# Layer 0's output stage re-stepped, its follow-ups queued, and root rows spread by transposes

## The chip, the cores and the metric

The kernel runs on one core of one Trainium2 chip. The metric is the device time of the program in microseconds (us); lower is better. TensorE (PE) does the matrix products, VectorE (DVE) and ScalarE (ACT) the elementwise work, SyncE (SP) issues the DMA transfers.

## The reference

Two layers of a mixer on 1024 latent tokens and 256 context tokens, width 1024. Each layer normalises its input, projects it with one large matrix, runs three branches (differential attention, a long convolution, a gated MLP), merges them, projects the merge with `w_out`, normalises that and adds it to the stream. What matters here is the end of layer 0 and the start of layer 1:

```python
h  = rms_norm(x,  norm_pre[l]) * (1.0 + sc) + sh      # start of a layer, latents
hc = rms_norm(xc, norm_pre[l]) * (1.0 + scc) + shc    # and context
...
out = merge_branches(z, (y_a, y_b, y_c), w_branch[l], w_out[l])
x_new = x + gt * rms_norm(out, norm_post[l])          # end of a layer, latents
xc = xc + gtc * rms_norm(outc, norm_post[l])          # and context, layer 0 only
```

Inside attention every head's output is normalised by the same kind of root mean square.

## The kernel before

**Layout.** Activations lie with channels on the 128 partitions and tokens along the free axis, in three chunks of tokens: chunk 0 and chunk 1 (512 latents each) and chunk 2 (256 context tokens). Every product is made of three single-pass products of split operands (`mm3`, L178): high part by high part, high by low, low by high. A weight block (128 output channels, all 1024 inputs) is loaded by SP into `wr` (two buffers, L83), its high part `wh` is copied by ACT (L100) and its low part `wl` is the difference, taken by DVE (L101); both have two buffers. `Weights.get` hands a block out, `Weights.ahead` splits the next one.

**Order of the work.** The program is written as generators that yield between pieces, and are stepped against each other by hand; a scheduler then fixes one list of instructions for each engine, and each engine runs its list in order. So an instruction that waits holds back all that stands behind it on its engine.

**Layer 0's output stage** (`phase_o`). `out(c)` makes, for one chunk, eight blocks of 128 output channels: 24 products on PE (tile `po`), a copy `ot` and a square by ACT (L1248, L1250) and a running sum of squares by DVE (L1252). The chunk's follow-up `tail(c)` then takes the root of the mean square (`mean_rsqrt_steps`, tiles `msq`, `mn`, `mrb`), scales `ot` (L1225), adds the old stream (`xt`, L1227), stores it, and makes the input of layer 1 from it: squares and their sum (`hroot_steps`, L323 and L325), a second root, and `hnorm_steps`: scaled copy `ht` (L344), high part `hh` by ACT (L346), low part `hl` by DVE (L347). The follow-up of a chunk is stepped once a block beside the products of the next chunk, and what is left of it is run off (`drain`) before the chunk after that. Its steps are large: four channel blocks of `ot` and `xt` at a time, eight squares in one step, four of `hnorm` in one step. Chunk 2 reuses the last two weight blocks and splits six new ones.

**The fills.** After chunk 2's products come three blocks of layer 1's input projection (`o_fill`, tile `pd`, result `zz` stored by SP), each for chunk 0 and then chunk 1, beside the follow-up of chunk 2. Layer 1's `phase_a` then loads its rotary tables (`ropeC`, `ropeS`, L553 and L554), and `kvq` makes the first head's keys (tile `pd` for chunks 0, 1 and 2), queries and values. The keys' results go through `rope` (L392 to L395) on DVE. In `phase_a` the tile `pd` has two buffers, so the third chunk's product waits for the first one's rotary step.

**Spreading a root.** `mean_rsqrt_steps` has the roots of 128 tokens as one column (`mn`); to have them along the free axis on all partitions it multiplies the column, repeated 128 times, by the identity (`mrb`, L215). Attention does that twice per 256 queries and head, the output stage four times per 512 tokens and root. `gate_row` in `phase_last` does the same with eight columns (L1325).

Of the kernel before, what the change touches and what calls it, by code (L numbers as in the profile page):

```python
# [166 lines left out]
class Kernel:  # L167
# [31 lines left out]
    def mean_rsqrt_steps(self, pool, psum, ss, n, width, tag="P"):  # L199


        nc = self.nc
        nt = n // 128
        ps = psum.tile([128, 512], F32, name="msq", tag=tag)
        for t in range(nt):
            nc.tensor.matmul(ps[:, 2 * t:2 * t + 2], lhsT=ss[:, 128 * t:128 * t + 128], rhs=self.ones[:, 0:2],
                             start=True, stop=True)
        m = pool.tile([128, 12], F32, name="mn", tag="mn", bufs=2)
        x, r, t = m[:, 0:nt], m[:, 4:4 + nt], m[:, 8:8 + nt]
        nc.vector.tensor_scalar(out=x, in0=ps[:, 0:2 * nt:2], scalar1=1.0 / width, scalar2=EPS, op0=MUL, op1=ADD)  # L210
        self.rsqrt(r, x, t)
        yield
        pr = psum.tile([128, 512], F32, name="mrb", tag=tag)
        for t in range(nt):
            nc.tensor.matmul(pr[:, 128 * t:128 * t + 128], lhsT=r[:, t:t + 1].to_broadcast([128, 128]), rhs=self.ident,  # L215
                             start=True, stop=True)
        return pr[:, 0:n]

    def chunks(self, l):
# [96 lines left out]
    def hroot_steps(self, c, xt, pool, psum, tag="P"):  # L316
        nc = self.nc
        n = CHUNKS[c][1]
        ss = pool.tile([128, 512], F32, name="ss", tag="ss")[:, 0:n]
        for k in range(KT):  # L320
            sq = ss if k == 0 else pool.tile([128, 512], F32, name="sq", tag="sq")[:, 0:n]
            for s, x in xt(k):
                nc.scalar.activation(out=sq[:, s], in_=x, func=AF.Square)  # L323
            if k:
                nc.vector.tensor_tensor(out=ss, in0=ss, in1=sq, op=ADD)  # L325
        yield
        return (yield from self.mean_rsqrt_steps(pool, psum, ss, n, D, tag))

    def hnorm_steps(self, l, c, xt, r, pool, tag=None):

        nc = self.nc
        n = CHUNKS[c][1]
        j = 1 if c == 2 else 0
        mod = self.mod[l, 0]
        hh, hl = self.alloc_h(c)
        for k in range(KT):
            if tag is None:
                t = pool.tile([128, 512], F32, name="ht", tag="sq")[:, 0:n]
            else:
                if k % 4 == 0:  # L340
                    t4 = pool.tile([128, 4, 512], F32, name="ht", tag=tag)
                t = t4[:, k % 4, 0:n]
            for s, x in xt(k):
                nc.vector.scalar_tensor_tensor(out=t[:, s], in0=x, scalar=mod[:, 8 + k, j:j + 1], in1=r[:, s],  # L344
                                               op0=MUL, op1=MUL)
            nc.scalar.activation(out=hh[:, k, :], in_=t, func=AF.Identity, bias=mod[:, k, j:j + 1])  # L346
            nc.vector.scalar_tensor_tensor(out=hl[:, k, :], in0=t, scalar=mod[:, k, j:j + 1],  # L347
                                           in1=hh[:, k, :].bitcast(F32), op0=ADD, op1=SUB)
            if k == 3:
                yield  # L350
        self.hT[c] = (hh, hl)

# [192 lines left out]
    def phase_a(self, l):  # L545
        nc = self.nc
        with ExitStack() as st:
            P = st.enter_context(self.tc.tile_pool(name=f"pa{l}", bufs=1, reuse_waits="tile"))
            psum = st.enter_context(self.tc.tile_pool(name=f"psa{l}", bufs=1, space=PSUM, reuse_waits="tile"))
            psum = PsumTags(psum, {"S": 1, "T": 2, "O": 1, "P": 2})  # L550
            self.ropeC = P.tile([128, SEQ], F32, name="ropeC")
            self.ropeS = P.tile([128, SEQ], F32, name="ropeS")
            nc.sync.dma_start(out=self.ropeC, in_=self.A["rope"][:, 0, :])  # L553
            nc.sync.dma_start(out=self.ropeS, in_=self.A["rope"][:, 1, :])  # L554

            rest = self.ada_rest(P) if l == 0 else iter(())
            for h in range(HEADS):
                drain(self.kvq(l, h, P, psum))
                fill = chain(*[self.block(("in", l, BLK_HY + b), self.chunks(l), psum, self.evac_z(P, self.zd[l], b))
                               for b in self.hy_fill[l][h]],  # L560
                             *[self.block(("in", l, BLK_GM + b), self.chunks(l), psum, self.evac_z(P, self.gm[l], b))
                               for b in (2 * h, 2 * h + 1)])
# [643 lines left out]
    def phase_o(self, l):  # L1206
        nc = self.nc
        gg = self.mod[l, 1]
        with ExitStack() as st:
# [5 lines left out]
            def tail(c, ot, ss):  # L1215
# [8 lines left out]
                for k in range(KT):  # L1224
                    nc.vector.scalar_tensor_tensor(out=ot[:, k, :], in0=ot[:, k, :], scalar=gg[:, k, j:j + 1], in1=r,  # L1225
                                                   op0=MUL, op1=MUL)
                    nc.vector.tensor_tensor(out=xt[:, k, :], in0=ot[:, k, :], in1=xt[:, k, :], op=ADD)  # L1227
                    if k % 4 == 3:
                        nc.sync.dma_start(out=dst[:, k - 3:k + 1, t0:t0 + n], in_=xt[:, k - 3:k + 1, :])
                        yield  # L1230
                xk = whole(xt)
                r = yield from self.hroot_steps(c, xk, P, psum, "N")
                yield from self.hnorm_steps(l + 1, c, xk, r, P)

            def out(c):
                t0, n = CHUNKS[c]
# [4 lines left out]
                for d in ds:  # L1241
                    w = self.ws.get(("out", l, c, d))
                    ps = psum.tile([128, 512], F32, name="po", tag="P")
                    for k in range(KT):
                        self.mm3(ps[:, 0:n], (w[0][:, k, :], w[1][:, k, :]), (mh[:, k, :], ml[:, k, :]),
                                 k == 0, k == KT - 1)
                    self.ws.ahead()
                    nc.scalar.activation(out=ot[:, d, :], in_=ps[:, 0:n], func=AF.Copy)  # L1248
                    sq = ss if d == ds[0] else P.tile([128, 512], F32, name="sq", tag="sq")[:, 0:n]
                    nc.scalar.activation(out=sq, in_=ps[:, 0:n], func=AF.Square)  # L1250
                    if d != ds[0]:
                        nc.vector.tensor_tensor(out=ss, in0=ss, in1=sq, op=ADD)  # L1252
# [4 lines left out]
            back = None  # L1257
            for c in self.chunks(l):
                for w in out(c):
                    if back is not None:  # L1260
                        next(back, None)
                drain(back)
                back = self.tails.pop()
            for b in self.o_fill:
                for i, w in enumerate(self.block(("in", l + 1, BLK_HY + b), self.chunks(l + 1), psum,
                                                 self.evac_z(P, self.zd[l + 1], b))):
# [14 lines left out]
    def phase_last(self, l):  # L1281
# [4 lines left out]
        with ExitStack() as st:  # L1286
# [34 lines left out]
            def gate_row():  # L1321
                for a in range(2):
                    ps = psum.tile([128, 512], F32, name="gr", tag="N")
                    for i in range(4):
                        nc.tensor.matmul(ps[:, 128 * i:128 * i + 128], rhs=self.ident, start=True, stop=True,  # L1325
                                         lhsT=gg[:, 4 * a + i, 0:1].to_broadcast([128, 128]))
# [55 lines left out]
    def order(self):  # L1382
        o = []
        o += [("in", 0, BLK_HY + b) for b in self.s_fill]
        for l in range(DEPTH):
            for h in range(HEADS):
                o += [("in", l, BLK_K + h), ("in", l, BLK_Q + h), ("in", l, BLK_V + h)]
                o += [("in", l, BLK_HY + b) for b in self.hy_fill[l][h]]
# [342 lines left out]
```

## Time and profile before

| | us |
|---|---|
| median of 3 runs | 3040.4 |
| lowest and highest | 3034.4 and 3042.98 |
| the profiled execution's own time | 3040.74 |
| its span (first to last instruction) | 3039.0 |
| PE busy / DVE busy / ACT busy in the span | 2964.2 / 1944.0 / 1225.0 |

Busy time of PE counts any matmul in flight; PE's clock has two levels, 1.2 and 2.4 GHz, and the profile gives the mean granted clock of a stretch as a share of the higher one. A float32 product with the identity shows as two weight loads and two matmul records, a transpose as one of each.

### The profile page before, as it was taken

Reading aid. Unit: us, or ns where it says so; the run is one execution under the profiler, and the core shown is the slowest. Engines: PE = TensorE matmul, PEld = TensorE weight load, DVE = VectorE, ACT = ScalarE, POOL = GpSimd, SP = SyncE. Lnnn points to the kernel's source line nnn. Section 1 sums busy time; section 2 is a strip of 40 time slices with the busy share of each in tenths; the row PEclk is TensorE's granted clock in tenths of the full one; section 3 lists DMA queues with packets and bytes.
Section 4 is the critical chain, followed back from the end, with each engine's and each line's share of the span. In section 5 each row is a group of like instructions: output and inputs, shape, how many; then the busy total and the mean of one; then the engine's idle time right before and its main releaser. Section 6 shows DMA issues by size and latency. Waiting matters only on the chain.

```text
span 3039.0 us, 43277 instructions
## 1 busy us (share of the span) xinstructions
PE 2964.2 (98%) x16220; PEld 2501.2 (82%) x16220; DVE 1944.0 (64%) x4458; ACT 1225.0 (40%) x2037; POOL 0.2 (0%) x4
## 2 busy tenths in 40 slices
PE   8999999999999999999999999999999999999998
PEld 4888888888888887888887788888887877788888
DVE  6856777777866766235657766566666877635464
ACT  4533535353532332233334444545455333223241
POOL 0000000000000000000000000000000000000000
PEclk9999999999999999999999999999999999999999
DMA  7324131313365656354443321111114756647342
GB/s 256 135 102 130 55 98 59 100 63 92 111 219 184 208 177 198 109 165 149 130 162 118 118 68 58 65 61 56 63 60 139 218 177 203 204 152 228 94 142 84
DMA packets 243378, 395.76 MB, mean 130 GB/s; under 512 B 23582, under 2 KB 127902, under 8 KB 241888
## 3 DMA queue, kind: packets, MB, share of 16 engines
q1 hardware_dynamic: 243168, 392.99, 40.1%
q8 instruction: 128, 2.10, 0.3%
q14 instruction: 82, 0.67, 0.1%
HBM read 285.81 MB, written 97.65 MB: 126 GB/s over the span
## 4 chain that ended last, share of the span: by engine, by line
PE 85%; DVE 7%; DMA 6%; ACT 1%; issue 1%; SPq 0%; DVEq 0%; ACTq 0%
PE pd L180 16%; PE pd L182 16%; PE pd L181 16%; PE S L452 5%; PE pb L181 3%; PE pb L182 3%; PE pb L180 3%; PE T L489 2%; PE po L182 2%; PE po L180 2%; PE po L181 2%; PE ip L703 2%; DMA aw<-in_ada_wT 2%; PE O L180 1%; PE O L181 1%; PE O L182 1%
## 5 line engine op out<-in xcount | busy, mean ns | idle before, releaser
L180 PE MATMUL pd<-hh,wh 128*128 128x512 f32 (+1 forms) x2784 | 1045.3, 376 | 9.0 <-DVE r L393 2.9
L181 PE MATMUL pd<-hl,wh 128*128 128x512 f32 (+1 forms) x2784 | 1031.5, 371 | 0.2 <-DVE hl L368 0.2
L182 PE MATMUL pd<-hh,wl 128*128 128x512 f32 (+1 forms) x2784 | 1029.3, 370 | 0.7 <-DVE wl L101 0.7
L180 PEld LDWEIGHTS pd<-hh,wh 128*128 128x128 f32 x2784 | 527.6, 190 | 89.9 <-issue 6.0
L182 PEld LDWEIGHTS pd<-hh,wl 128*128 128x128 f32 x2784 | 527.1, 189 | 84.6 <-DVE wl L101 1.6
L181 PEld LDWEIGHTS pd<-hl,wh 128*128 128x128 f32 x2784 | 528.2, 190 | 77.1 <-issue 0.9
L101 DVE TENSOR_TENSOR wl<-wr,wh 128x1024 fp32r<-128x1024 f32 (+1 forms) x204 | 223.6, 1096 | 209.6 <-ACT wh L100 206.0
L100 ACT ACTIVATE wh<-wr 128x1024 fp32r<-128x1024 f32 (+1 forms) x204 | 195.2, 957 | 286.7 <-PE pd L181 182.1
L459 ACT ACTIVATE e<-S,sm 128x1280 f32<-128x1280 f32 (+1 forms) x144 | 177.7, 1234 | 178.0 <-DVE sm L457 143.8
L456 DVE TENSOR_REDUCE sm<-S 128x1 f32<-128x1280 f32 (+1 forms) x144 | 197.2, 1369 | 67.8 <-PE S L452 67.2
L180 PE MATMUL pb<-gh,wh 128*128 128x512 f32 (+1 forms) x480 | 177.4, 370 | 1.3 <-ACT gh L196 1.3
L181 PE MATMUL pb<-gl,wh 128*128 128x512 f32 (+1 forms) x480 | 177.7, 370 | 0.4 <-DVE gl L197 0.3
L182 PE MATMUL pb<-gh,wl 128*128 128x512 f32 (+1 forms) x480 | 177.3, 369 | 0.0
L452 PE MATMUL S<-K,q 128*128 128x512 f32 (+1 forms) x400 | 149.1, 373 | 6.9 <-ACT e L459 6.8
L1045 ACT ACTIVATE ev<-pd 128x512 f32<-128x512 f32 (+1 forms) x122 | 66.7, 546 | 170.8 <-PE pd L182 113.7
L452 PE MATMUL S<-K,w 128*128 128x512 f32 (+1 forms) x400 | 135.3, 353 | 0.0
L197 DVE TENSOR_TENSOR pl<-T,ph 128x512 fp32r<-128x512 f32 x164 | 109.5, 687 | 28.1 <-ACT ph L196 26.3
L196 ACT ACTIVATE ph<-T 128x512 fp32r<-128x512 f32 x164 | 94.3, 597 | 67.9 <-PE T L489 67.8
L290 DVE SCALAR_TENSOR_TENSOR at<-aw,acs 128x256 f32<-128x256 f32 x224 | 88.5, 421 | 40.6 <-DMA aw<-in_ada_wT 37.9
L468 DVE SCALAR_TENSOR_TENSOR e<-e,sm,e 128x1280 f32<-128x1280 f32 (+1 forms) x72 | 102.7, 1426 | 6.2 <-ACT e L467 5.7
L452 PEld LDWEIGHTS S<-K,q 128*128 128x128 f32 x400 | 75.0, 187 | 38.3 <-ACT e L459 24.7
L489 PE MATMUL T<-ident,e 128*128 128x128 f32 x656 | 104.3, 276 | 0.6 <-DVE pl L197 0.3
(390 smaller groups left out, 4594.9 us busy)
## 6 DMA issues: line engine op xcount, KB each, us to landing
wr<-in_w_in SPq DMA_DIRECT2D x136, 512.0 KB, 3.5
fm<-in_fmat SPq DMA_DIRECT2D x99, 192.0 KB, 3.1
fm<-in_imat SPq DMA_DIRECT2D x72, 256.0 KB, 2.9
sel<-sd SPq DMA_DIRECT2D x70, 256.0 KB, 2.7
aw<-in_ada_wT SPq DMA_DIRECT2D x128, 128.0 KB, 2.5
wr<-in_w_out SPq DMA_DIRECT2D x28, 512.0 KB, 3.3
sd<-ev SPq DMA_DIRECT2D x50, 256.0 KB, 2.3
zd<-zz SPq DMA_DIRECT2D x48, 256.0 KB, 2.0
```

Of the source, the lines that this page charges most:

```text
L100: nc.scalar.activation(out=hi[:, 0:k, :], in_=t[:, 0:k, :], func=AF.Copy)
L101: nc.vector.tensor_tensor(out=lo[:, 0:k, :], in0=t[:, 0:k, :], in1=hi[:, 0:k, :].bitcast(F32), op=SUB)
L180: mm(out, lhsT=wh, rhs=xh, start=first, stop=False)
L181: mm(out, lhsT=wh, rhs=xl, start=False, stop=False)
L182: mm(out, lhsT=wl, rhs=xh, start=False, stop=last)
L196: nc.scalar.activation(out=hi, in_=src, func=AF.Copy)
L197: nc.vector.tensor_tensor(out=lo, in0=src, in1=hi.bitcast(F32), op=SUB)
L452: nc.tensor.matmul(S[:, a - k0:b - k0], lhsT=st[:, o + 128 * t:o + 128 * t + 128], rhs=K[m][:, a:b], start=i == 0, stop=i == 1)
L456: nc.vector.reduce_max(out=sm[:, 0:1], in_=S[:, 0:nk], axis=AX.X)
L459: nc.scalar.activation(out=e[:, 0:nk], in_=S[:, 0:nk], func=AF.Exp, bias=sm[:, 1:2], scale=0.125, accum_out=sm[:, 2:3])
L468: nc.vector.scalar_tensor_tensor(out=e0[:, 0:nk], in0=e0[:, 0:nk], scalar=s0[:, 3:4], in1=e[:, 0:nk], op0=MUL, op1=ADD)
L489: nc.tensor.transpose(T[:, 256 * i + 128 * t:256 * i + 128 * t + 128], e[t][:, 128 * (2 * g + i):128 * (2 * g + i) + 128], self.ident)
```

## The change

Five edits, all in the order or the form of the work, none in its results:

1. `mrb` and `gate_row` spread their columns with `nc.tensor.transpose` in place of `nc.tensor.matmul`.
2. In layer 0's output stage the follow-ups of the chunks yield more often (two channel blocks in place of four, squares in steps of two, `hnorm` in steps of two), wait in a queue `backs`, and are stepped twice a block beside chunks 0 and 1 and once a block beside chunk 2. Nothing is drained between chunks.
3. `ahead()` stands in front of a block's products, not behind them.
4. The first two fills do chunk 0 first, then the queue is run down to chunk 2's follow-up, then the rest of the fills.
5. In layer 1, the first convolution block of head 0's fills (block 7) comes ahead of the head's keys.

```diff
@@ mean_rsqrt_steps
-            nc.tensor.matmul(pr[:, 128 * t:128 * t + 128], lhsT=r[:, t:t + 1].to_broadcast([128, 128]), rhs=self.ident,
-                             start=True, stop=True)
+            nc.tensor.transpose(pr[:, 128 * t:128 * t + 128], r[:, t:t + 1].to_broadcast([128, 128]), self.ident)
@@ hroot_steps
-        yield
+            if k % every == every - 1:
+                yield
@@ hnorm_steps
-            if k == 3:
+            if k % every == every - 1 and k < KT - 1:
                 yield
@@ phase_a
+                hy = [self.block(("in", l, BLK_HY + b), self.chunks(l), psum, self.evac_z(P, self.zd[l], b))
+                      for b in self.hy_fill[l][h]]
+                if l > 0 and h == 0:
+                    drain(hy.pop(0))
                 drain(self.kvq(l, h, P, psum))
...
@@ phase_o, tail
                     if k % 4 == 3:
                         nc.sync.dma_start(out=dst[:, k - 3:k + 1, t0:t0 + n], in_=xt[:, k - 3:k + 1, :])
+                    if k % 2:
                         yield
...
-                r = yield from self.hroot_steps(c, xk, P, psum, "N")
-                yield from self.hnorm_steps(l + 1, c, xk, r, P)
+                r = yield from self.hroot_steps(c, xk, P, psum, "N", 2)
+                yield from self.hnorm_steps(l + 1, c, xk, r, P, every=2)
@@ phase_o, out
+                    self.ws.ahead()
                     for k in range(KT):
                         self.mm3(...)
-                    self.ws.ahead()
+                        if k == 3:
+                            yield 2.6 * n / 512
...
-                    yield 5.2 * n / 512
+                    yield 2.6 * n / 512
@@ phase_o, stepping
             for c in self.chunks(l):
-                for w in out(c):
-                    if back is not None:
-                        next(back, None)
-                drain(back)
-                back = self.tails.pop()
-            for b in self.o_fill:
-                for i, w in enumerate(self.block(...)):
-                    if i % 4 == 1:
-                        next(back, None)
-            drain(back)
+                for i, w in enumerate(out(c)):
+                    if c < 2 or i % 2 == 0:
+                        step()
+                backs.append(self.tails.pop())
+            fills = [self.block(...) for b in self.o_fill]
+            for a, b in (fills[0:2],):
+                for i in range(4):
+                    next(a)
+                    step()
+                for i in range(4):
+                    next(b)
+                    step()
+            while len(backs) > 1:
+                step()
+            for f in fills:
+                for w in f:
+                    step()
+            while backs:
+                step()
```

Beside chunk 2's products DVE's list reads as follows before: `ss` is chunk 2's own sum, `ot` and `xt` are chunk 1's follow-up, `wl` the low part of a weight block of chunk 2.

```order
L1252 TENSOR_TENSOR ss<-ss,sq 128x256
L1225 SCALAR_TENSOR_TENSOR ot<-ot,mod_4467,mrb 128x512 x2
L1227 TENSOR_TENSOR xt<-ot,xt 128x512 x2
L1225 SCALAR_TENSOR_TENSOR ot<-ot,mod_4467,mrb 128x512 x2
L1227 TENSOR_TENSOR xt<-ot,xt 128x512 x2
L101 TENSOR_TENSOR wl<-wr,wh 128x1024
```

And now, at the same place:

```order
L1258 TENSOR_TENSOR ss<-ss,sq 128x256
L1228 SCALAR_TENSOR_TENSOR ot<-ot,mod_4467,mrb 128x512 x2
L1230 TENSOR_TENSOR xt<-ot,xt 128x512 x2
L1258 TENSOR_TENSOR ss<-ss,sq 128x256
L101 TENSOR_TENSOR wl<-wr,wh 128x1024
```

Four operations of the follow-up stand between two weight splits where there were eight.

At the end of the stage SP's list reads before (`wr` are weight blocks of layer 1, `w` are copies that head 0's queries need):

```order
L542 DMA zd_71<-zz 128x512 x2
L83 DMA wr<-in_w_in 128x1024
L553 DMA ropeC<-in_rope 128x1024
L554 DMA ropeS<-in_rope 128x1024
L83 DMA wr<-in_w_in 128x1024
L430 DMA w_16605<-q_16603 64x512 x2
```

And now:

```order
L542 DMA zd_71<-zz 128x512
L83 DMA wr<-in_w_in 128x1024
L553 DMA ropeC<-in_rope 128x1024
L554 DMA ropeS<-in_rope 128x1024
L542 DMA zd_71<-zz 128x512 x2
L83 DMA wr<-in_w_in 128x1024 x2
```

The rotary tables stand ahead of the two stores of the block that has moved in front of the keys, where they stood behind all stores of the fills.

## Rows read from the trace of the kernel before

**Rows 1.** Page: busy time of PE, its share of the span, records.

```profile
PE 2964.2 (98%) x16220; PEld 2501.2 (82%) x16220; DVE 1944.0 (64%) x4458; ACT 1225.0 (40%) x2037; POOL 0.2 (0%) x4
```

**Rows 2.** Busy time by stage: stretch, length, PE, PEld, DVE, ACT, POOL, clock, DMA.

```profile
1552.07:1595.60 43.53, 43.53 (x194) 36.06 (x193) 14.42 (x18) 15.18 (x23) 0.00 (x0) 1.00 0.51 181
1595.60:1644.85 49.25, 48.20 (x226) 39.30 (x224) 34.03 (x65) 21.06 (x33) 0.00 (x0) 1.00 0.31 107
1644.85:1685.54 40.69, 32.36 (x217) 31.07 (x216) 34.03 (x62) 19.74 (x36) 0.00 (x0) 0.83 0.47 155
1685.54:1736.97 51.43, 47.38 (x219) 38.28 (x217) 36.79 (x93) 19.66 (x36) 0.00 (x0) 0.99 0.36 123
1736.97:1743.17 6.20, 6.20 (x26) 5.86 (x27) 4.92 (x9) 1.26 (x2) 0.00 (x0) 0.50 0.01 3
```

**Rows 3.** Waits of PE, 1540 to 1740: us in total, times, longest.

```profile
PE po L180 <- ACT wh L100: 5.7, 4, 3.2
PE po L182 <- DVE wl L101: 3.5, 3, 2.8
```

**Rows 4.** Timeline of PE: start, length, work, and idle time before it.

```profile
1666.01 0.58 PE L182 MATMUL po<-hh,wl 128*128 128x256 f32 x1 [2.79 <-DVE wl L101]
...
1736.97 0.55 PE L180 MATMUL pd<-hh,wh 128*128 128x256 f32 x1 [2.89 <-DVE r L393]
```

**Rows 5.** Timeline of PE at the end of chunk 2's products, 14 records between.

```profile
1683.74 0.28 PE L180 MATMUL po<-hh,wh 128*128 128x256 f32 x1
...
1685.54 0.40 PE L180 MATMUL pd<-hh,wh 128*128 128x512 f32 x1
```

**Rows 6.** Timeline of DVE beside chunk 2's products and after them.

```profile
1655.37 0.16 DVE L190 TENSOR_TENSOR mn<-mn 128x4 f32<-128x4 f32 x1
...
1662.21 1.40 DVE L1225 SCALAR_TENSOR_TENSOR ot<-ot,mod,mrb 128x512 f32<-128x512 f32 x2
1663.53 1.29 DVE L1227 TENSOR_TENSOR xt<-ot,xt 128x512 f32<-128x512 f32 x2
1664.73 1.22 DVE L101 TENSOR_TENSOR wl<-wr,wh 128x1024 fp32r<-128x1024 f32 x1
1665.87 0.42 DVE L1252 TENSOR_TENSOR ss<-ss,sq 128x256 f32<-128x256 f32 x1
1666.20 1.40 DVE L1225 SCALAR_TENSOR_TENSOR ot<-ot,mod,mrb 128x512 f32<-128x512 f32 x2
...
1690.28 2.07 DVE L347 SCALAR_TENSOR_TENSOR hl<-ht,mod,hh 128x512 fp32r<-128x512 f32 x3
```

**Rows 7.** Records of `mrb` in four stretches (columns PE, PEld, DVE, clock), then of `gr`.

```profile
250.00:850.00 600.00, 12.65 (x80) 10.55 (x80) 9.51 (x20) 1.00 0.28 88
1552.00:1743.00 191.00, 5.67 (x40) 5.07 (x40) 29.33 (x48) 0.95 0.39 135
1743.00:2340.00 597.00, 10.19 (x64) 8.77 (x64) 7.67 (x16) 1.00 0.22 69
2940.00:3039.00 99.00, 1.05 (x8) 0.97 (x8) 5.60 (x8) 0.97 0.29 96
...
2970.00:2990.00 20.00, 1.95 (x16) 1.94 (x16) 1.20 (x2) 1.00 0.02 5
```

**Rows 8.** Timeline of PE in attention: a root spread, then transposes.

```profile
315.17 0.60 PE L215 MATMUL mrb<-ident,mn 128*128 128x128 f32 x4
315.61 0.27 PE L489 MATMUL T<-ident,e 128*128 128x128 f32 x1
...
1798.23 0.60 PE L489 MATMUL T<-ident,e 128*128 128x128 f32 x4
```

**Rows 9.** Timeline of SP's queue at the rotary tables.

```profile
1730.48 0.42 SPq L553 DMA_DIRECT2D ropeC<-in_rope  x1
```

**Rows 10.** Longest wait of PE, 250 to 850; then a stretch late in layer 1's head 0.

```profile
PE S L452 <- ACT e L459: 6.8, 5, 2.3
...
1900.00:1910.00 10.00, 10.00 (x60) 8.82 (x59) 2.06 (x3) 2.67 (x6) 0.00 (x0) 1.00 0.36 107
```

More of the change, by code (lines that the diff above doesn't have):

```diff
@@ L314, in alloc_h, with hroot_steps @@
                 self.hp.tile([128, KT, n], F32R, name=f"hl{c}", tag=f"hl{c}"))
-    def hroot_steps(self, c, xt, pool, psum, tag="P"):
+    def hroot_steps(self, c, xt, pool, psum, tag="P", every=KT):
         nc = self.nc
@@ L325, in hroot_steps, with hnorm_steps @@
                 nc.vector.tensor_tensor(out=ss, in0=ss, in1=sq, op=ADD)
-        yield
+            if k % every == every - 1:
+                yield
         return (yield from self.mean_rsqrt_steps(pool, psum, ss, n, D, tag))
-    def hnorm_steps(self, l, c, xt, r, pool, tag=None):
+    def hnorm_steps(self, l, c, xt, r, pool, tag=None, every=4):
         nc = self.nc
@@ L557, in phase_a @@
             for h in range(HEADS):
+                hy = [self.block(("in", l, BLK_HY + b), self.chunks(l), psum, self.evac_z(P, self.zd[l], b))
+                      for b in self.hy_fill[l][h]]
+                if l > 0 and h == 0:
+                    drain(hy.pop(0))
                 drain(self.kvq(l, h, P, psum))
-                fill = chain(*[self.block(("in", l, BLK_HY + b), self.chunks(l), psum, self.evac_z(P, self.zd[l], b))
-                               for b in self.hy_fill[l][h]],
+                fill = chain(*hy,
                              *[self.block(("in", l, BLK_GM + b), self.chunks(l), psum, self.evac_z(P, self.gm[l], b))
@@ L1252, in out, with step @@
                         nc.vector.tensor_tensor(out=ss, in0=ss, in1=sq, op=ADD)
-                    yield 5.2 * n / 512
+                    yield 2.6 * n / 512
                 self.tails.append(tail(c, ot, ss))
             self.tails = []
-            back = None
-            for c in self.chunks(l):
-                for w in out(c):
-                    if back is not None:
-                        next(back, None)
-                drain(back)
-                back = self.tails.pop()
-            for b in self.o_fill:
-                for i, w in enumerate(self.block(("in", l + 1, BLK_HY + b), self.chunks(l + 1), psum,
-                                                 self.evac_z(P, self.zd[l + 1], b))):
-                    if i % 4 == 1:
-                        next(back, None)
-            drain(back)
+            backs = []
+            def step():
+                while backs:
+                    try:
+                        return next(backs[0])
+                    except StopIteration:
+                        backs.pop(0)
+            for c in self.chunks(l):
+                for i, w in enumerate(out(c)):
+                    if c < 2 or i % 2 == 0:
+                        step()
+                backs.append(self.tails.pop())
+            fills = [self.block(("in", l + 1, BLK_HY + b), self.chunks(l + 1), psum, self.evac_z(P, self.zd[l + 1], b))
+                     for b in self.o_fill]
+            for a, b in (fills[0:2],):
[10 more added lines that the diff above has]
+                    step()
+            while backs:
+                step()
     def place_out(self, key):
@@ L1324, in gate_row @@
                     for i in range(4):
-                        nc.tensor.matmul(ps[:, 128 * i:128 * i + 128], rhs=self.ident, start=True, stop=True,
-                                         lhsT=gg[:, 4 * a + i, 0:1].to_broadcast([128, 128]))
+                        nc.tensor.transpose(ps[:, 128 * i:128 * i + 128],
+                                            gg[:, 4 * a + i, 0:1].to_broadcast([128, 128]), self.ident)
                     nc.scalar.activation(out=row[:, 512 * a:512 * a + 512], in_=ps, func=AF.Copy)
@@ L1386, in order @@
             for h in range(HEADS):
+                n = 1 if l > 0 and h == 0 else 0
+                o += [("in", l, BLK_HY + b) for b in self.hy_fill[l][h][:n]]
                 o += [("in", l, BLK_K + h), ("in", l, BLK_Q + h), ("in", l, BLK_V + h)]
-                o += [("in", l, BLK_HY + b) for b in self.hy_fill[l][h]]
+                o += [("in", l, BLK_HY + b) for b in self.hy_fill[l][h][n:]]
                 o += [("in", l, BLK_GM + b) for b in (2 * h, 2 * h + 1)]
```

## The prediction

> **What bounds the kernel now.** The page comes first: PE is busy for 2964.2 us of a span of 3039.0, DVE for 1944.0 [rows 1]. So time is won where PE is given less to do, or where it stands idle or runs at its lower clock. The view by stage tells where the latter is [rows 2]. I cut the output stage at PE's own landmarks: chunk 0's products, chunk 1's, chunk 2's, the three fills with the first two key products, and the key product of chunk 2. Chunk 0 is clean: 192 wide products in 43.53 us, 0.227 each, clock 1.00. Chunk 1 has the same 192 and takes 49.25. Chunk 2 has 192 products of half the width and takes 40.69, with PE busy for 32.36 of it and the clock at 0.83. The fills take 51.43, and the last piece, 24 narrow products, 6.20 at a clock of 0.50.
>
> The waits of PE name the cause in chunk 2: the weight halves `wh` and `wl` come late [rows 3]. The timeline shows the longest one, 2.79 us for `wl`, and another kind of 2.89 us for the rotary step [rows 4]. DVE's timeline shows why `wl` is late: four `ot` and four `xt` of chunk 1's follow-up stand ahead of it [rows 6]. A narrow product costs 0.12 (15 in 1.80 us [rows 5]), so a block of 24 lasts 2.88 us on PE, while DVE needs from pair to pair 1.32 for `ot`, 1.20 for `xt`, 1.14 for `wl`, 0.33 for `ss` [rows 6]: 2 x (1.32 + 1.20) + 1.14 + 0.33 = 6.5 for one such step. PE must wait.
>
> **Part 1, roots by transposes.** In attention a root's spread shows 80 records in layer 0 and 64 in layer 1, 40 in the output stage, 8 in the last stage, and `gr` 16 [rows 7]; two records a product, so 40, 32, 20, 4 and 8 products. Four records take 315.17 to 315.61, 0.11 each, and four transposes last just as long, 0.60 with the drain, at one record each [rows 8]. So each product loses one record of 0.11: 72 in attention give 7.9 us, 20 in the output stage 2.2, 12 in the last stage 1.3; the first stage has another 10 by the code (4, 4 and 2 for the chunks), which partly lie beside waits, 0.6. Sum 12.0. In attention it counts in full only where PE is the bound. Layer 1 shows PE busy without a gap late in head 0 [rows 10]; layer 0's longest wait sums to 6.8 us in 600 [rows 10], and less work on PE could lengthen it, at most by layer 0's own share of 4.4, at least by nothing. I take 0, the busy rows being nearer.
>
> **Part 2, what the output stage loses today.** Chunk 1: 43.5 plus four root products of eight records, 4 x 0.9, is 47.1; it takes 49.25, a loss of 2.1. Chunk 2: 192 x 0.12 = 23.0 and three roots, 2.7, make 25.7; loss 15.0. Fills: 192 x 0.227 = 43.5 and roots of 2.7 make 46.2; loss 5.2. The last piece: 24 x 0.12 = 2.9; loss 3.3. Together 25.6 us, of which 13.4 are idle (length less busy in [rows 2]) and the rest lower clock and handshakes after it: 1.9 us lost for each us of idle.
>
> **Part 3, what it will lose.** Follow-ups now come in pairs, as DVE's order shows. Beside chunk 2 one block meets 1.32 + 1.20 + 1.14 + 0.33 = 3.99 on DVE against 2.88 on PE. That is still too much, by 1.1, and four weight blocks follow such a step: 4.4 us idle. A check over the whole stretch: from chunk 0's root to chunk 1's last `hl` DVE has 8 pairs of `ot` (10.6) and of `xt` (9.6), 14 sums of squares at `xt`'s 0.60 (8.4), 32 `ht` and `hl`, all at the 0.69 of an `hl` (22.1 [rows 6]), 14 `wl` (16.0), 7 wide and 7 narrow `ss` (6.5) and five root chains of ten at 0.16 (8.0): 81.2. PE has in that stretch, by the order now, 168 wide products (38.1), 192 narrow (23.0), 69 of the fills (15.6) and 5.0 of roots: 81.7. The two are level, so nothing is hidden with room to spare, and 4.4 of stall is what I would expect, not none. Priced as today, at 1.9, that is a loss of 8.4. Gain: 25.6 - 8.4 = 17.2.
>
> The fills in the new order want chunk 0's `hh` and `hl` for 48 products, 10.9 us, while DVE ends chunk 1's; that is in the check. Splitting a block ahead moves `wh` in ACT's list, but two buffers bound it as before (ACT has 19.74 busy of 40.69 in chunk 2 [rows 2]): I count nothing. More steps issue no more DMAs.
>
> **Part 4, the rotary tables.** They are issued at 1730.48 [rows 9], too late for the first key product; hence the 2.89 us and the 0.50 clock after it. Now a block of 48 products, 10.9 us, stands between. In SP's list the tables stay behind one weight load and go ahead of that block's stores. If the load held them as long as today, 10.9 still covers 2.89. This part is inside the 17.2.
>
> **Part 5, head 0 gets one block less.** The block of 10.9 us is only moved. If head 0 runs out of it near its end, PE waits on scores or on transposes; the bounds are 0 and the longest kind of wait of layer 0, 6.8 for a whole layer [rows 10]. I take 1.
>
> **Sum.** 12.0 + 17.2 - 1 = 28.2; 3040.7 for the profiled execution less 28.2 is 3012.5. That execution stands 0.3 above the median of 3040.4, so no correction.
>
> **The rivals.**
> *All stalls vanish*: DVE keeps up, the 8.4 go too: 3004. For it, the level sums above; against it, 3.99 against 2.88.
> *Chunk 2 stays slow*: a few idle us bring the clock down as in [rows 2], and its 15.0 stay lost with the fills' waits cured. Loss 17 in place of 8.4: 3021. For it, that 8.3 us of idle in chunk 2 today go with a clock of 0.83; against it, that a slower PE lets DVE catch up.
> *The transposes save nothing*: a repeated column keeps two records. Then 12.0 is missing: 3024.5. Against it, all transposes in [rows 8] show one.
> *Slower*: PE's clock falls after a root that is spread by transposes. The price is that of the last piece, 6.20 us for what costs 2.9 at the full clock: 3.3 a fall. Attention spreads 36 roots: 36 x 3.3 = 119 less 28, 3131. It ends slower from nine falls on. Against it, attention with its many transposes stands at 1.00 [rows 7]. The Trainium skill has a rule for this rival (TensorE: Matmul & The Clock Gate, section "PE-mode transpose"): transposes do not count as work for the full clock. By that rule the time would be above the old one; this trace disagrees where transposes lie between other products, with 1.00 over 600 us [rows 7].
>
> **How the numbers follow.** The forecast has 0.60, all stalls vanishing 0.15, chunk 2 staying slow 0.16, no saving by transposes 0.05, the falling clock 0.03, several at once 0.01. The range takes in the first four: 3003 to 3025. What a measurement of this kernel can tell from no change is about 0.3%, 9.1 us, so faster means below 3031.3. The first three cases are there, and the fourth almost surely: 0.92. Within 0.3%: 0.05, if two bad ones meet. Slower: 0.03.
>
> **What would show it.** Right: `mrb` with 106 records where there were 212, `gr` with 8; chunk 2's products in some 30 to 34 us with waits for `wl` of about 1 us each; the key product of chunk 2 at a clock of 1.00 and no wait for `ropeC`; layer 1's attention without new waits of PE. Wrong: a clock under 1.00 in the heads, `wl` waits as long as today, a wait for chunk 1's `hl` in the fills that is longer than 3 us, or head 0's end with idle of more than 5 us.

## The result and the profile after

The changed kernel takes 3007.5 us (median of four runs, 3006.33 to 3008.97), the kernel before 3040.13 beside it: a ratio of 0.9899, 95% interval 0.9882 to 0.9916. The forecast was 3012.5, range 3003 to 3025. The profiled execution took 3006.53, its span is 3004.8, so 34.2 us went out of the span. One of the four executions of the kernel *without transposes* below took 9867 us, and stands in neither its median nor its ratio.

The page first; it answers to [rows 1]:

```profile
PE 2943.0 (98%) x16106; PEld 2481.0 (83%) x16106; DVE 1944.2 (65%) x4458; ACT 1223.5 (41%) x2037; POOL 0.2 (0%) x4
```

PE has 114 records and 21.2 us of busy time less; DVE and ACT did the same work as before, to 1.5 us. So DVE's work was moved and not reduced.

The output stage, cut at the same landmarks as [rows 2] (stretch, length, busy time of PE, PEld, DVE, ACT, POOL, granted clock, DMA share, GB/s). The fourth stretch now holds the 48 products of the moved block as well:

```profile
1547.52:1591.05 43.53, 43.53 (x194) 36.04 (x193) 15.00 (x19) 15.38 (x23) 0.00 (x0) 1.00 0.51 182
1591.05:1638.80 47.75, 47.10 (x218) 38.36 (x216) 37.53 (x71) 22.73 (x36) 0.00 (x0) 1.00 0.33 110
1638.80:1666.92 28.12, 25.36 (x205) 24.55 (x204) 26.50 (x48) 15.83 (x29) 0.00 (x0) 1.00 0.63 210
1666.92:1726.15 59.23, 57.98 (x266) 47.33 (x265) 44.76 (x107) 25.19 (x45) 0.00 (x0) 1.00 0.39 132
1726.15:1729.03 2.88, 2.88 (x26) 2.87 (x25) 2.60 (x5) 0.00 (x0) 0.00 (x0) 1.00 0.00 0
```

Chunk 2's products went from 40.69 to 28.12, the last key product from 6.20 to 2.88, and the clock is at 1.00 everywhere. The five stretches add up to 181.51; before they were 191.10, and 202.0 with the moved block's 10.9. The output stage gave 20.5.

PE's waits from 1547 to 1730 (total us, times, longest), against [rows 3]:

```profile
PE po L182 <- DVE wl L101: 2.8, 4, 0.9
PE mrb L215 <- DVE mn L192: 0.8, 1, 0.8
PE po L180 <- ACT wh L100: 0.5, 1, 0.5
PE msq L206 <- DVE ss L324: 0.4, 1, 0.4
```

The four waits for `wl` in PE's timeline (start, length, work, idle before it), where [rows 4] had one of 2.79:

```profile
1652.22 0.38 PE L182 MATMUL po<-hh,wl 128*128 128x256 f32 x1 [0.20 <-DVE wl L101]
1656.21 0.39 PE L182 MATMUL po<-hh,wl 128*128 128x256 f32 x1 [0.85 <-DVE wl L101]
1660.20 0.39 PE L182 MATMUL po<-hh,wl 128*128 128x256 f32 x1 [0.85 <-DVE wl L101]
1664.19 0.39 PE L182 MATMUL po<-hh,wl 128*128 128x256 f32 x1 [0.85 <-DVE wl L101]
```

They are 3.99 us apart. DVE's timeline between two splits, against [rows 6], shows the cycle behind that:

```profile
1658.93 1.22 DVE L101 TENSOR_TENSOR wl<-wr,wh 128x1024 fp32r<-128x1024 f32 x1
1660.06 1.40 DVE L1228 SCALAR_TENSOR_TENSOR ot<-ot,mod,mrb 128x512 f32<-128x512 f32 x2
1661.38 1.29 DVE L1230 TENSOR_TENSOR xt<-ot,xt 128x512 f32<-128x512 f32 x2
1662.58 0.42 DVE L1258 TENSOR_TENSOR ss<-ss,sq 128x256 f32<-128x256 f32 x1
1662.92 1.22 DVE L101 TENSOR_TENSOR wl<-wr,wh 128x1024 fp32r<-128x1024 f32 x1
```

DVE has no wait between 1646.61 and 1665.08, so here it sets the pace of PE, one weight block per 3.99 us.

The records of the spread roots in the whole kernel (ns shortest/middle/longest, first to last in us, shape):

```profile
L215 PE MATMUL mrb<-ident,mn x106: 270/272/476, 35.0 to 2952.7; 128*128 128x128 f32 x106
...
L1348 PE MATMUL gr<-ident,mod x8: 271/272/273, 2944.8 to 2945.6; 128*128 128x128 f32 x8
```

One record each, 106 and 8. In layer 1's attention a spread and the wide product behind it read so:

```profile
1796.34 0.38 PE L215 MATMUL mrb<-ident,mn 128*128 128x128 f32 x2
1796.47 0.47 PE L180 MATMUL pd<-hh,wh 128*128 128x512 f32 x1
```

A spread of two products has two records where it had four. The wide product behind it starts 0.13 after the first of them and the one after that 0.45 after it (1796.79); less the 0.23 of a wide product that is 0.22 for the two records, where four took 0.44 [rows 8]. Last, SP's queue at the rotary tables, against [rows 9]:

```profile
1707.19 0.42 SPq L553 DMA_DIRECT2D ropeC<-in_rope  x1
```

It is issued 19 us ahead of the key product of chunk 2 (1726.15); before it was 6.5, and 2.9 of these were PE's wait.

**Where the 34 us came from**, by stretches between landmarks that both traces have. Two groups of records serve as landmarks besides the stage: `mm` (the first product of what follows attention in each layer) and `pb` (the branches' products). Before:

```profile
L1096 PE MATMUL mm<-wsT,ones x32: 272/273/323, 861.6 to 2320.1; 128*64 128x128 f32 x32
...
L182 PE MATMUL pb<-gh,wl x480: 279/389/628, 1327.7 to 2933.9; 128*128 128x512 f32 x136, 128*128 128x256 f32 x24
```

And after:

```profile
L1099 PE MATMUL mm<-wsT,ones x32: 272/273/324, 857.6 to 2290.8; 128*64 128x128 f32 x32
...
L182 PE MATMUL pb<-gh,wl x480: 279/389/628, 1320.7 to 2901.1; 128*128 128x512 f32 x136, 128*128 128x256 f32 x24
```

| stretch | before | after | change | forecast |
|---|---|---|---|---|
| start to first `mm` | 861.6 | 857.6 | -4.0 | -5.0 |
| first `mm` to first `pb` | 466.1 | 463.1 | -3.0 | 0 |
| first `pb` to first `po` | 224.4 | 226.8 | +2.4 | 0 |
| output stage with the moved block | 202.0 | 181.5 | -20.5 | -19.4 |
| to layer 1's last `mm`, without the moved block | 566.0 | 561.7 | -4.3 | -2.5 |
| last `mm` to last `pb` | 613.8 | 610.3 | -3.5 | 0 |
| last `pb` to the end | 105.1 | 103.7 | -1.4 | -1.3 |

The change touches nothing in the three rows forecast at 0. Over the twelve traces besides that of before they run from 462.4 to 465.8, from 222.0 to 226.8 and from 608.5 to 615.2, so a single pair of traces can't place some 4 us of the difference.

### The profile page after: what moved, and what is told of

Its sections match the earlier page's. It is cut to its first block, busy times and chain, and to the rows that moved or that the text cites. A ratio compares the mean times of both kernels' runs of the same rounds, so it can differ in the third digit from the quotient of the medians.

```text
span 3004.8 us, 43059 instructions
## 1 busy us (share of the span) xinstructions
PE 2943.0 (98%) x16106; PEld 2481.0 (83%) x16106; DVE 1944.2 (65%) x4458; ACT 1223.5 (41%) x2037; POOL 0.2 (0%) x4
## 4 chain that ended last, share of the span: by engine, by line
PE 86%; DVE 6%; DMA 5%; issue 1%; ACT 1%; SPq 0%; DVEq 0%; ACTq 0%
PE pd L182 16%; PE pd L180 16%; PE pd L181 16%; PE S L452 5%; PE pb L181 3%; PE pb L180 3%; PE pb L182 3%; PE T L489 2%; PE po L180 2%; PE po L182 2%; PE po L181 2%; PE ip L706 2%; DMA aw<-in_ada_wT 2%; PE O L180 1%; PE O L181 1%; PE O L182 1%
## 5 line engine op out<-in xcount | busy, mean ns | idle before, releaser
L541 ACT ACTIVATE zz<-pd 128x512 f32<-128x512 f32 (+1 forms) x126 | 68.8, 546 | 93.1 <-PE pd L182 92.9
L180 PEld LDWEIGHTS pb<-gh,wh 128*128 128x128 f32 x480 | 91.3, 190 | 18.1 <-ACT gh L196 2.5
```

The costliest lines, as they stand in the source:

```text
L180: mm(out, lhsT=wh, rhs=xh, start=first, stop=False)
```

## The experiments

Three groups of kernels ran, each on another chip than the pair above; the kernel before took 3029.51, 3032.88 and 3031.75 there. So ratios are compared, and stages of the traces. "Stage" is from the first `po` to the end of chunk 2's key product; where the moved block does not lie in it, its 10.9 us are added.

| kernel | median | ratio to before | 95% interval | stage |
|---|---|---|---|---|
| before | | 1 | | 202.0 |
| change | 3007.5 | 0.9899 | 0.9882 to 0.9916 | 181.5 |
| transposes alone | 3019.21 | 0.9968 | 0.9954 to 0.9982 | 198.0 |
| without transposes | 3017.91 | 0.9955 | 0.9939 to 0.9972 | 183.2 |
| keys first | 3003.24 | 0.9915 | 0.99 to 0.9929 | 181.6 |
| block ahead alone | 3026.46 | 0.998 | 0.9969 to 0.9991 | 194.4 |
| split behind | 3010.23 | 0.9935 | 0.992 to 0.9949 | 186.2 |
| fills block by block | 3007.98 | 0.992 | 0.9905 to 0.9934 | 186.1 |
| coarse steps | 3023.73 | 0.9972 | 0.9962 to 0.9981 | 202.5 |
| step every other block | 3011.09 | 0.9932 | 0.9917 to 0.9947 | 189.1 |
| add on GpSimd | 3006.66 | 0.9918 | 0.9903 to 0.9932 | 184.1 |
| add left out | 2999.83 | 0.9894 | 0.9878 to 0.991 | 178.9 |
| change again | 3003.5 | 0.9906 | 0.9887 to 0.9926 | 181.5 |

The last row bears the others: the unchanged change on another chip has the same stage to the tenth, while whole runs spread by more than the 4 or 5 us that some parts are worth. Such parts are therefore read from the stage.

### Roots by transposes: alone, and the change without them

Edit 1 alone in the kernel before:

```diff
@@ mean_rsqrt_steps, kernel before; likewise in gate_row
-            nc.tensor.matmul(pr[:, 128 * t:128 * t + 128], lhsT=r[:, t:t + 1].to_broadcast([128, 128]), rhs=self.ident,
-                             start=True, stop=True)
+            nc.tensor.transpose(pr[:, 128 * t:128 * t + 128], r[:, t:t + 1].to_broadcast([128, 128]), self.ident)
```

> The kernel before with only the root spreads and the gate row as transposes. My theory: mrb shows 106 records and gr 8, each of 114 products loses 0.11 us, 10 to 12.5 us in all, so 3028 to 3030, and the output stage keeps its 190 us less 2. Rival one: the record saved was hidden in the weight loads beside it, and the time stays at 3040. Rival two: PE's clock falls behind the transposes, over 3050.

Measured 0.9968, 10.3 us between the medians. `mrb` has one record per product, and the stalls of the output stage stayed (chunk 2's products):

```profile
1637.28:1675.42 38.14, 30.30 (x214) 29.09 (x213) 33.91 (x62) 19.38 (x36) 0.00 (x0) 0.87 0.49 166
```

The key product behind the fills also waits as before, 3.4 us for the rotary step. The stage is 4.0 shorter, 2 more than was counted.

The reverse edit in the changed kernel:

```diff
@@ mean_rsqrt_steps, changed kernel; likewise in gate_row
-            nc.tensor.transpose(pr[:, 128 * t:128 * t + 128], r[:, t:t + 1].to_broadcast([128, 128]), self.ident)
+            nc.tensor.matmul(pr[:, 128 * t:128 * t + 128], lhsT=r[:, t:t + 1].to_broadcast([128, 128]), rhs=self.ident,
+                             start=True, stop=True)
```

> The changed kernel with the spreads as products again. My theory: the two parts add up, so 12 us over the changed kernel, 3018 to 3020. Rival: with the output stage no longer stalling or with attention having holes, one part hides the other, and it is under 3014 or over 3025.

Measured 0.9955, with two records a product again:

```profile
L215 PE MATMUL mrb<-ident,mn x212: 270/275/422, 36.6 to 2964.0; 128*128 128x128 f32 x106
```

By stretches it loses 3.8 up to the first `mm`, 1.7 in the output stage, 5.1 in layer 1's attention and 1.3 at the end: 11.9 us. The first of these is read between two chips, and the changed kernel itself has 857.6 and 854.1 there in its two traces; so the sum holds to some 3.5 us. Both ways the edit is worth about what was counted.

### The block ahead of the keys: left out, and alone

```diff
@@ phase_a and order(), changed kernel
-                if l > 0 and h == 0:
+                if False:
                     drain(hy.pop(0))
...
-                n = 1 if l > 0 and h == 0 else 0
+                n = 0
```

> The changed kernel with block 7 back behind head 0's keys. As the prediction has it (part 4), that block is what covers the rotary tables: without it the wait of 2.9 us for them and the low clock behind it come back, 5 to 6 us, 3013. Rival, from the trace of the changed kernel: the tables are now issued at 1707.2 because the follow-ups end earlier, and land some 3 us after the first key product would end without the block, while chunk 1's key product still keeps PE busy for 5.4: no wait, 0 to 1.5 us, 3007.5 to 3009.

The stage is the same to 0.1, and no wait of PE for the rotary step came back: the rival held. The fills and the last key product:

```profile
1661.85:1710.21 48.36, 47.14 (x219) 38.32 (x217) 42.05 (x105) 22.54 (x42) 0.00 (x0) 1.00 0.40 139
1710.21:1713.08 2.87, 2.87 (x26) 2.85 (x24) 2.81 (x6) 0.62 (x1) 0.00 (x0) 1.00 0.00 0
```

The tables were issued at 1700.79, 9.4 us ahead of that key product, without any block between. So beside the other edits the moved block is worth nothing. Is it of no use at all, or does something else do its work? Edit 5 alone in the kernel before:

```diff
@@ phase_a and order(), kernel before
+                if l > 0 and h == 0:
+                    drain(hy.pop(0))
                 drain(self.kvq(l, h, P, psum))
...
+                n = 1 if l > 0 and h == 0 else 0
```

> The kernel before with only block 7 moved ahead of head 0's keys. My theory: here the rotary tables are late (issued at 1730.5 beside the first key product), so the 10.9 us of the block cover them, the wait of 2.9 us and the low clock behind it go, 5 to 6 us less than before; so the block is a second remedy for a wait that the finer steps also cure, and worth nothing beside them. Rival: the load that the tables stand behind moves back with the block, the wait stays, and the time is that of before within 1 us.

Measured 0.998, 5.3 us between the medians, as expected. Chunk 2's products and the last key product:

```profile
1639.90:1679.45 39.55, 31.40 (x217) 30.02 (x216) 34.03 (x62) 19.85 (x36) 0.00 (x0) 0.87 0.47 160
...
1738.70:1741.57 2.87, 2.87 (x26) 2.87 (x24) 2.60 (x5) 0.00 (x0) 0.00 (x0) 1.00 0.00 0
```

The key product has its 2.87 at the full clock while chunk 2 still stalls. The same stall has two cures in this change, and either is enough.

### The split ahead of a block's products

```diff
@@ phase_o, out, changed kernel
-                    self.ws.ahead()
                     for k in range(KT):
...
+                    self.ws.ahead()
                     nc.scalar.activation(out=ot[:, d, :], in_=ps[:, 0:n], func=AF.Copy)
```

> The changed kernel with the next split asked for behind a block's products, as before. My theory: two buffers bound the split, so where it is asked for moves nothing: within 1.5 us of the changed kernel, and the four waits for wl in chunk 2 stay at about 0.9 us. Rival: the split falls behind a block's own copy and square on ACT beside chunk 2, waits of PE for wh come back there, 3 to 8 us more.

Chunk 0 and 1 together, then chunk 2:

```profile
1544.09:1636.25 92.16, 91.16 (x411) 74.27 (x409) 52.80 (x90) 38.07 (x59) 0.00 (x0) 1.00 0.40 143
1636.25:1668.50 32.25, 28.31 (x206) 27.47 (x204) 26.29 (x48) 15.62 (x29) 0.00 (x0) 0.89 0.58 196
```

The stage is 4.7 longer, where at most 1.5 was expected, and 4.1 of it lie beside chunk 2. PE's waits there:

```profile
PE po L182 <- DVE wl L101: 2.6, 2, 1.4
PE po L180 <- ACT wh L100: 1.4, 2, 0.8
```

They sum to 4.0 against 2.8 in the change, the longest is 1.4 against 0.9, and the clock goes to 0.89. The rival is not the reason: beside chunk 2 ACT's list has the same operations in the same order in both kernels. DVE's list has changed. Each split now stands behind the pair of the follow-up that is stepped in the middle of its block, so two pairs come ahead of the first late one:

```profile
1648.39 1.41 DVE L1228 SCALAR_TENSOR_TENSOR ot<-ot,mod,mrb 128x512 f32<-128x512 f32 x2
1649.71 1.29 DVE L1230 TENSOR_TENSOR xt<-ot,xt 128x512 f32<-128x512 f32 x2
1650.91 1.22 DVE L101 TENSOR_TENSOR wl<-wr,wh 128x1024 fp32r<-128x1024 f32 x1
```

This split starts 14.66 us after the first product of chunk 2, in the change 12.14 (1650.94): later by one pair, 1.32 + 1.20. The load behind it is issued when it has ended (1652.20, in the change 1652.22), so that much later too, and the second wait for `wh` (0.55) is for the block which that load brings. What the first (0.84) hangs on was not found.

### The order of the fills

```diff
@@ phase_o, stepping, changed kernel
-            for a, b in (fills[0:2],):
...
             while len(backs) > 1:
                 step()
```

The loop taken out is the one that does chunk 0 first in two fills.

> The changed kernel with the fills one block after the other, chunk 0 then chunk 1, and chunk 1's follow-up run down ahead of them. My theory: PE comes to chunk 1's fill 5.4 us earlier and waits there for the root and hl of chunk 1, which DVE cannot bring sooner: 4 to 6 us more than the changed kernel, some 3012.5, with waits for hl, hh or mrb of 4 us or more and a lower clock behind them. Rival: DVE has room there, under 1.5 us.

The fills with the moved block took 63.77 in place of 59.23:

```profile
1665.39:1729.16 63.77, 61.18 (x266) 49.42 (x265) 44.73 (x107) 25.43 (x45) 0.00 (x0) 0.95 0.37 122
```

The loss is as expected, 4.6 over the stage, but no wait of 4 us is there. The longest is for chunk 1's `hh`, which the first fill wants too early:

```profile
PE pd L180 <- ACT hh L346: 1.3, 1, 1.3
```

Only 1.3 us more idle than in the change (2.59 against 1.25) stand in that stretch; the other 3.2 are PE busy for longer, at a clock of 0.95.

### The size of a step

```diff
@@ phase_o, tail, changed kernel
-                    if k % 2:
+                    if k % 4 == 3:
                         yield
...
-                r = yield from self.hroot_steps(c, xk, P, psum, "N", 2)
-                yield from self.hnorm_steps(l + 1, c, xk, r, P, every=2)
+                r = yield from self.hroot_steps(c, xk, P, psum, "N")
+                yield from self.hnorm_steps(l + 1, c, xk, r, P)
```

> The changed kernel with the follow-up in its old large steps (four channel blocks, eight squares, four of hnorm at a time) but still queued. My theory: beside chunk 2 a block then meets 6.5 us of DVE work against 2.9 on PE; one wait of about 2.8 to 3.6 us per large step, the clock falls as before, and 6 to 12 us come back: 3013 to 3019. Rival: the queue alone does it, since the follow-up no longer has to end with the chunk; within 2 us.

The stage is 202.5: 21.0 longer, where 6 to 12 was expected, and as slow as the kernel before. With large steps some of chunk 1's products fall behind the landmark, so the two stretches are taken together:

```profile
1540.63:1630.77 90.14, 84.01 (x367) 67.80 (x365) 50.00 (x88) 37.32 (x58) 0.00 (x0) 0.95 0.37 135
1630.77:1681.56 50.79, 43.25 (x257) 39.36 (x258) 33.72 (x64) 18.65 (x34) 0.00 (x0) 0.84 0.43 145
```

140.93 against 119.40 in the change and 133.47 in the kernel before [rows 2]; PE is idle for 13.7 of it, against 3.4 and 9.4. DVE's timeline shows the old cycle, eight operations of the follow-up ahead of a split:

```profile
1656.18 1.41 DVE L1228 SCALAR_TENSOR_TENSOR ot<-ot,mod,mrb 128x512 f32<-128x512 f32 x2 [0.47 <-PE mrb L215]
1657.50 1.29 DVE L1230 TENSOR_TENSOR xt<-ot,xt 128x512 f32<-128x512 f32 x2
1658.70 1.40 DVE L1228 SCALAR_TENSOR_TENSOR ot<-ot,mod,mrb 128x512 f32<-128x512 f32 x2
1660.02 1.29 DVE L1230 TENSOR_TENSOR xt<-ot,xt 128x512 f32<-128x512 f32 x2
...
1661.56 1.22 DVE L101 TENSOR_TENSOR wl<-wr,wh 128x1024 fp32r<-128x1024 f32 x1
```

So the gain of the stage hangs on the step size: queue, split ahead, fill order, moved block and transposes together gain nothing there while the steps are large. They even lose 7.5 us beside the three chunks' products, where chunk 1 now stalls too, and win most of it back behind them. The other half was not tried: small steps in the old order, without the queue.

### How often to step

Beside chunk 2 a step every other block, in place of every block:

```diff
@@ phase_o, stepping, changed kernel
-                    if c < 2 or i % 2 == 0:
+                    if c < 2 or i % 4 == 0:
                         step()
```

> The changed kernel with a step of the follow-up at every other block beside chunk 2. DVE then has 5.46 us for two blocks of 5.76 on PE, so the four waits of 0.85 us for wl go. My theory, from the sums that were level (81.2 us of DVE, 81.7 of PE): what is not done beside chunk 2 is late in the fills, and the 2.8 us come back there as waits for chunk 1's hl or mrb: within 2 us of the changed kernel. Rival: there is room in the fills, and it is 2 to 3 us faster, 3005.

Chunk 2's products, then the fills with the moved block:

```profile
1637.36:1662.15 24.79, 24.59 (x206) 24.38 (x204) 20.28 (x39) 14.06 (x26) 0.00 (x0) 1.00 0.50 171
1662.15:1732.35 70.20, 63.39 (x267) 50.07 (x265) 50.98 (x116) 27.52 (x48) 0.00 (x0) 0.93 0.39 135
```

Chunk 2 became free of stalls, 3.3 us shorter, and the fills lost 11.0: PE waited 4.5 us in two pieces for a late root (`mn`), and the clock was 0.93. That the work comes back in the fills was expected; that it costs more than it saved, 7.6 us over the stage, was not.

### Relief for DVE beside chunk 2

Chunk 1's eight adds of the old stream on GpSimd:

```diff
@@ phase_o, tail, changed kernel
-                    nc.vector.tensor_tensor(out=xt[:, k, :], in0=ot[:, k, :], in1=xt[:, k, :], op=ADD)
+                    (nc.gpsimd if c == 1 else nc.vector).tensor_tensor(out=xt[:, k, :], in0=ot[:, k, :], in1=xt[:, k, :], op=ADD)
```

> The changed kernel with the eight additions xt = ot + xt of chunk 1's follow-up on GpSimd, which is idle. DVE then has 2.79 us a block beside chunk 2 against 2.88 on PE. My theory: DVE's work was what the waits for wl came from, so they go, and 2.8 us or somewhat more are won: 3004 to 3005. Rival: the two engines hold each other up or GpSimd is several times slower, chunk 1's follow-up ends later, and it is 0 to 8 us slower.

Chunk 2's products became 2.5 longer, not shorter, as the rival had it:

```profile
1636.29:1666.88 30.59, 26.35 (x206) 25.94 (x204) 27.47 (x40) 15.83 (x29) 12.54 (x8) 0.94 0.60 204
```

DVE lost eight operations and is busy for longer (27.47 against 26.50). Its timeline beside GpSimd's shows two kinds of operation stretched:

```profile
1650.20 1.39 DVE L1228 SCALAR_TENSOR_TENSOR ot<-ot,mod,mrb 128x512 f32<-128x512 f32 x2
1651.52 2.24 DVE L101 TENSOR_TENSOR wl<-wr,wh 128x1024 fp32r<-128x1024 f32 x1
1653.68 1.51 DVE L1258 TENSOR_TENSOR ss<-ss,sq 128x256 f32<-128x256 f32 x1
...
1646.46 8.45 POOL L1230 TENSOR_TENSOR xt<-ot,xt 128x512 f32<-128x512 f32 x5 [1646.02 <-DVE ot L1228]
```

Whether DVE's work sets chunk 2's pace is thus not answered by this run. A probe without the eight adds answers it:

```diff
@@ phase_o, tail, changed kernel
-                    nc.vector.tensor_tensor(out=xt[:, k, :], in0=ot[:, k, :], in1=xt[:, k, :], op=ADD)
+                    if c != 1:
+                        nc.vector.tensor_tensor(out=xt[:, k, :], in0=ot[:, k, :], in1=xt[:, k, :], op=ADD)
```

> The changed kernel with the eight additions xt = ot + xt of chunk 1's follow-up left out (chunk 1 then goes into layer 1 without its update, so this is no version, only a probe). DVE has 2.79 us a block beside chunk 2 against 2.88 on PE, and no second engine is in its way. My theory: the four waits for wl of chunk 2 go, its products take 24.5 to 25.5 us in place of 28.12, and as chunk 1's follow-up is 4.8 us shorter nothing comes back in the fills: 2.5 to 3.5 us less than the changed kernel. Rival: what keeps wl late is ACT's wh or the two buffers, and the waits stay at 0.85.

```profile
1635.39:1660.71 25.32, 24.59 (x205) 24.39 (x204) 21.26 (x39) 15.85 (x29) 0.00 (x0) 1.00 0.50 167
```

Chunk 2 takes 25.32, 2.8 less, and the fills 59.39, 0.2 more. PE's waits for `wl` fell from 2.8 to 0.7: DVE's cycle of 3.99 was their cause.

### The change once more

No edit; the changed kernel on the chip of the last group.

> The changed kernel once more, on the chip of the two runs beside it, so that they can be set against it: its stages as before within 0.3 us (chunk 2's products 28.1, fills with the moved block 59.2), its ratio to the kernel before 0.988 to 0.992.

Measured 0.9906 (28.3 us between the medians), the four stretches 91.30, 28.12, 59.22 and 2.87. None of the variants that do all the work is clearly faster than the change: keys first has 0.9915 and the same stage.

## Why the prediction held, and where it did not

**Part 1, transposes: right.** 12.0 forecast, 11.9 found by leaving the edit out, to some 3.5 us, and 10.3 by trying it alone. Layer 1's attention gained 4.3 (5.1 were lost there without the edit), more than the 3.5 counted and with no hole in it.

**Part 3, the new stall: the mechanism and the loss per block exact, the price wrong, the place too narrow.** DVE's cycle of 3.99 us was worked out from [rows 6] and is the distance of the four waits. PE is idle for 0.85 of it, but it loses the 1.11 of the prediction (3.99 less 2.88): the last product before a wait still runs out and the first one behind it starts slowly, 0.26 together, which the profile counts as busy. Three blocks lose 1.11 each, the first one, with 0.20 idle, some 0.4: 3.7, which is the whole loss of chunk 2 (28.12 against 24.4, the prediction's clean figure with its 12 records less). So 4.4 was nearly right as it stood, and the step that failed is "priced as today, at 1.9", which made 8.4 of it. That price holds the lower clock of the kernel before, 0.83 with waits of up to 3.2 [rows 2, 3]; here the clock stayed at 1.00. The sign "some 30 to 34 us" for chunk 2 failed with it.

Over the whole stage the same count gives 163.2 as clean (165.4 less 2.2) and 170.6 measured, a loss of 7.4 against 8.4. The other 3.7 lie in chunk 1 and the fills, which the forecast took as cleared; 1.9 of it is idle, the rest PE busy for longer than the clean figure. Two errors of opposite sign made the sum good: 20.5 for the stage, 19.4 forecast. That is luck.

The check that the sums are level was a little too kind: it takes a root chain on DVE as ten operations of 0.16, where the trace has eleven, one each 0.20 (1644.10 to 1646.08 in the changed kernel). Five chains are then 11 and not 8, and DVE's 81.2 becomes 84, above PE's 81.7.

**"I count nothing" for the split ahead: wrong.** It is worth 4.7. The reason given, that two buffers bound the split, looked at ACT's list, where indeed nothing moves. What decides is DVE's list: asked for behind the products, a split comes one pair of the follow-up later, and the clock goes to 0.89.

**Part 4, the rotary tables: the outcome right, the cause only one of two.** In the kernel before the rotary step waits for the table itself, which lands 5.6 us after its issue:

```profile
1736.13 0.69 DVE L393 TENSOR_TENSOR r<-pd,ropeC 128x512 f32<-128x512 f32 x1 [4.61 <-DMA ropeC<-in_rope]
```

The moved block covers that, as forecast, when it is the only edit. In the changed kernel it is not needed: without it the tables are issued 9.4 us before the product that needs their step, where in the kernel before that product, held up by 2.9, started 6.5 after the issue. The transposes are not the second cure, since alone they leave a wait of 3.4. Which of steps, split and fill order it is was not tried apart.

**Part 5, head 0: the hole did not come.** The longest wait of PE in layer 1's attention is 0.2.

**The rivals.** *All stalls vanish* and *chunk 2 stays slow* both fell with 28.12 against a clean 24.4 and an old 40.69; the second was no idle fear, since coarse steps in the queue take as long as the old stage. *No saving by transposes* fell with 106 records. *Slower* needed nine falls of the clock: the granted clock is 1.00 over layer 1's attention with its 32 spread products:

```profile
1729.03:2290.80 561.77, 561.43 (x3036) 467.90 (x3034) 354.75 (x687) 275.22 (x410) 0.00 (x0) 1.00 0.20 64
```

The Trainium skill's rule that transposes do not count as work for the full clock (TensorE: Matmul & The Clock Gate, section "PE-mode transpose") is not tested here for transposes alone, since no run has such a kernel; where they lie between other products, as in this stretch, the clock stayed at 1.00.

**The 5 us between 3012.5 and 3007.5.** Some 4 of the 6 us that the span lost beyond the forecast lie in stretches that the change does not touch. On the last chip the change took 28.3 off, the forecast's 28.2. That the rest is the spread of runs is likely but was not shown.

**The parts do not add up.** Left out one at a time in the output stage, the steps cost 21.0, the split 4.7, the fill order 4.6, the transposes 1.7 and the block 0.1, together 32.1, where all of them gain 20.5. Put alone into the kernel before, with its large steps, the block gains 7.6 there and the transposes 4.0. So a part's worth depends on what stands beside it: the block gains 7.6 alone and 0.1 beside the others. Small steps, split and fill order were not tried alone.

## What to carry to other kernels

A follow-up that shares an engine with the feed of the bound engine should come in steps whose time, with the feed's own, is about the bound engine's period: here 3.99 against 2.88 lost 3.7 us a chunk where 6.5 lost 15 [rows 2]. Fewer steps at that place are no cure if the work comes due right behind it. Before a part of a change is credited with a gain, leave it out and try it alone: two cures for one stall each look useful or useless, according to which is tried first.

## What the runs showed of the hardware

**DVE and GpSimd held each other up.** With GpSimd adding 128x512 tiles beside it, DVE's running sum took 1.51 in place of 0.42 and its weight split 2.24 in place of 1.22, while `ot` stayed at 1.39 for two. GpSimd's eight adds took from 1.28 to 2.28 us each, where DVE does two in 1.29. The one that started second was held: the split of 1647.56, begun just before an add of 1647.7, took 1.29 and that add 2.28; the split of 1651.52, begun behind an add of 1651.4, took 2.24 and that add 1.28. The operations that were stretched read both inputs from SBUF; `ot` has one of its inputs, `mrb`, in PSUM. The Trainium skill says just that (SBUF — State Buffer, section "Who interferes with whom"): a DVE operation with two inputs from SBUF contends with a GpSimd operation that reads SBUF, one with at most one such input, outside DVE's two-port modes, does not. The trace agrees, 1.51 against 0.42 and 1.39 against 1.40, so an add that reads SBUF was no relief for DVE on GpSimd here, where DVE splits weights.

**An idle microsecond has no fixed price.** Four waits of at most 0.85, one per 3.99 us and 2.8 in all, went with a clock of 1.00, and cost 0.26 each beyond the idle time. With the split behind, waits of 0.84 and 1.38 with two products between were followed by 3.2 us at the lower level (0.50 over 1652.19 to 1655.40), 0.89 over chunk 2. Beside GpSimd a single wait of 1.43 was followed by 1.00 (1653.82 to 1656.50) and one of 2.82 by 0.54 (1659.77 to 1663.00), 0.94 over chunk 2. The kernel before has 8.3 us of idle there, in waits of up to 3.2, and 0.83 [rows 2, 3]. Neither the sum of the idle time nor the longest wait alone puts these rows in order.
